# A third exponential, in place over the scores in PSUM, as the source of the remainder in the first layer

## The chip, the cores and the metric

The kernel runs on one core of one Trainium2 chip. The metric is device time in microseconds (us) for one execution of the whole program, as the median of several runs. The engines are named as the profile names them: PE (matmul) and PEld (the weight loads of the same engine), DVE (VectorE), ACT (ScalarE), POOL (GpSimd) and SP (which issues DMAs).

## The reference

One inference step of a two-layer encoder trunk, for a prompt of 2048 new frames and a sample of 32 frames. The first layer mixes tokens by attention within a band of 64-frame chunks, with a learned relative-position bias; the second by multi-head latent attention. The part that the change touches is the first layer's attention, 16 heads of 64:

```python
def attend(q, k, v, bias, mask, scale):
    s = jnp.einsum('bqhd,bkhd->bhqk', q, k).astype(jnp.float32) * scale
    if bias is not None:
        s = s + bias[None]
    s = jnp.where(mask[None, None], s, NEG_INF)
    p = jax.nn.softmax(s, axis=-1).astype(v.dtype)
    return jnp.einsum('bhqk,bkhd->bqhd', p, v)
```

A chunk sees itself and the eight chunks before it. All is float32, so the kernel splits every factor of a matmul in two float32r parts, a high one (the rounded value) and a low one (the remainder), and adds the products.

## The kernel before, in words

The first layer goes over 32 steps: two halves of the prompt, in each eight pairs of heads (`g`), for each pair two blocks of 512 queries (`blk`). A step handles two heads (`h`). Each head goes over tiles of 128 keys against up to 512 queries: four tiles (`c` = 1, of widths 512, 384, 256 and 128) in block 0, and eight in the later blocks, where four tiles of the block before come in (`c` = 0, of the same four widths). That makes 8 items in each of the 8 steps of block 0 and 16 in each of the other 24, 448 items in all, 112 of each width, 320 columns wide on average.

An item is made in `scores`. Two matmuls (L629 and L630) write the transposed scores into a PSUM bank; the tag `st` has two banks, bank_74 and bank_78, which items take in turn. The second matmul subtracts the row maximum, which `prep` found before. DVE adds the bias in place (L633, for some tiles L636) and masks a corner with a memset (L637). ACT then reads the bank twice: P = exp as float32 into SBUF (L643; for a head's first item straight into the sum `acc`) and Ph = exp rounded to float32r (L644). DVE forms the remainder Pl = P - Ph (L645) out of these two SBUF tiles, and POOL adds P to `acc` (L647) for all but a head's first item. P, Ph and Pl have three buffers each.

In `values`, two items later (`LAGA` = 2), one matmul multiplies Ph (L656) and one Pl (L657) by the values, into the one bank of the tag `av` (bank_94). After a head's last item `evac` takes that bank out (ACT L666, DVE L667) and folds the two halves of `acc` (DVE L668). `finish` makes the denominators: a matmul with `half_ones`, a product with 1 + exp(-z), and four reciprocals on DVE (L687), then two multiplications (L688, L689).

Beside these items stands the work for the next step: `project` and `project_z` (the matmuls of L189, L190 and L191), `prep` (transposes, the split of queries and keys by ACT L562 and L564 and DVE L566 and L567, the row maxima on DVE, L595 and L613), `finish` of the step before, and weight splits. A plan places them between the items in the program, and a scheduler then sets the order on each engine when the program is built: it goes by the program's order and by what is ready in its own account, so an instruction that waits longer there lets others pass. On the chip each engine runs its list in that order.

The buffers of P, Ph and Pl are named with numbers: P@63 to P@65, Ph@55 to Ph@57, Pl@58 to Pl@60; `acc` is acc@61 and acc@62.

Of the kernel before, what the change touches and what calls it, by code (L numbers as in the profile page):

```python
# [10 lines left out]
AF = mybir.ActivationFunctionType  # L11
ALU = mybir.AluOpType
# [19 lines left out]
def f32(ap):  # L32
    return ap if ap.dtype == F32 else ap.bitcast(F32)
# [6 lines left out]
def flip(t, c0, c1):  # L40

    n = t.shape[1]
    a = t[:, n - c1:n - c0]
    return bass.AP(a.tensor, a.offset + c1 - c0 - 1, [list(a.ap[0]), [-1, c1 - c0]])
# [55 lines left out]
def trunk(ctx: ExitStack, tc: tile.TileContext, I, O, stop=99):  # L100
    nc = tc.nc
    V, S, G, T = nc.vector, nc.scalar, nc.gpsimd, nc.tensor
# [90 lines left out]
    def bank(tag):  # L193
        order = psum[tag if tag in psum else "mx"]
        order.append(order.pop(0))
        return banks[order[-1]]
# [144 lines left out]
    def at1(shape, name, dt=F32, bufs=1):  # L341
        return at.tile(shape, dt, tag=name, name=name, bufs=bufs)
# [279 lines left out]
    def scores(s, h, n, c, t):  # L622
        blk, u = s["blk"], s[h]
        src = blk % 2 if c else 1 - blk % 2
        q0, w = (128 * t, 512 - 128 * t) if c else (0, 128 * t + 128)
        ks, qs = slice(128 * t, 128 * t + 128), slice(q0, q0 + w)
        bt = bias[s["g"], h][1]
        st = bank("st")
        T.matmul(st[:, 0:w], KA[h][src][:, ks], u["qa"][:, qs], start=True, stop=False)  # L629
        T.matmul(st[:, 0:w], KG[h][src][:, ks], u["qg"][:, qs], start=False, stop=True)  # L630
        if c:
            b1 = min(256, w)
            V.tensor_tensor(st[:, 0:b1], st[:, 0:b1], flip(bt, 0, b1), ALU.add)  # L633
        else:
            if t == 3:
                V.tensor_tensor(st[:, 0:128], st[:, 0:128], flip(bt, 128, 256), ALU.add)  # L636
            V.memset(st[0:64, w - 64:w], NEG)  # L637
        Ph = at1([128, 512], "Ph", F32R, PBUFS)
        Pl = at1([128, 512], "Pl", F32R, PBUFS)
        if n == 0:  # L640
            u["acc"] = at1([128, 512], "acc", bufs=2)
        P = at1([128, 512], "P", bufs=PBUFS) if n else u["acc"]
        S.activation(P[:, 0:w], st[:, 0:w], AF.Exp)  # L643
        S.activation(Ph[:, 0:w], st[:, 0:w], AF.Exp)  # L644
        V.tensor_tensor(Pl[:, 0:w], P[:, 0:w], f32(Ph[:, 0:w]), ALU.subtract)  # L645
        if n:
            G.tensor_tensor(u["acc"][:, qs], u["acc"][:, qs], P[:, 0:w], ALU.add)  # L647
        return Ph, Pl, w, qs, src
# [289 lines left out]
    for si, s in enumerate(steps):  # L938
# [55 lines left out]
        for i, (h, n, c, t) in enumerate(items):  # L994
            fifo.append((s, h, n, n == len(tiles) - 1, t, scores(s, h, n, c, t)))
            while plan and plan[0][0] <= (i + 1) / len(items):
                next(plan.pop(0)[1], None)
            if len(fifo) > LAGA:
                x = fifo.pop(0)
                values(*x)  # L1000
                if x[3]:
                    evac(x[0], x[1])
# [725 lines left out]
    for i in range(len(items) + LAG + 20):  # L1728
        if i < len(items):
            u, t = items[i]  # L1730
            fifo.append((u, t, scores(u, t)))
# [233 lines left out]
```

## Time and profile before

| what | us |
|---|---|
| median of 3 runs | 3829.01 |
| lowest, highest | 3823.49, 3842.70 |
| the profiled execution's own time | 3833.15 |
| its span, first to last instruction | 3831.0 |
| PE busy, all of the span | 3573.2 |
| DVE busy | 2996.9 |
| ACT busy | 1987.3 |
| POOL busy | 1629.8 |

The first layer's items run from about 130 to 1680 us of the span, and the rows below are nearly all of that stretch, called the stage. Two things have to be kept in mind when they are read. Matmuls are pipelined and their records overlap, so a busy PE is not PE at its peak. And a wait is put down to the semaphore that came last.

### The profile page before, as it was taken

Reading aid. Unit: us, or ns where it says so; the run is one execution under the profiler, and the core shown is the slowest. Engines: PE = TensorE matmul, PEld = TensorE weight load, DVE = VectorE, ACT = ScalarE, POOL = GpSimd, SP = SyncE. Lnnn points to the kernel's source line nnn. Section 1 sums busy time; section 2 is a strip of 40 time slices with the busy share of each in tenths; the row PEclk is TensorE's granted clock in tenths of the full one; section 3 lists DMA queues with packets and bytes.
Section 4 is the critical chain, followed back from the end, with each engine's and each line's share of the span. In section 5 each row is a group of like instructions: output and inputs, shape, how many; then the busy total and the mean of one; then the engine's idle time right before and its main releaser. Section 6 shows DMA issues by size and latency. Waiting matters only on the chain. (4 is left out here: it accounts for less than half of the span.)

```text
span 3831.0 us, 56760 instructions
## 1 busy us (share of the span) xinstructions
PE 3573.2 (93%) x17810; PEld 2892.2 (75%) x17810; DVE 2996.9 (78%) x6694; ACT 1987.3 (52%) x4790; POOL 1629.8 (43%) x1680
## 2 busy tenths in 40 slices
PE   7899999989999999889998999978999999998999
PEld 4678878777776667667887888857777787777887
DVE  4788888879988877877777766678888898885653
ACT  3544544555444434552223555546767677775542
POOL 0132222333333323541112444448788888885032
PEclk9899999989999999889999999979999999999999
DMA  5222222222223332343446476663332332333253
GB/s 172 68 60 59 65 77 67 72 70 67 64 82 98 105 89 76 98 145 123 132 132 209 143 203 195 189 166 112 90 92 70 96 89 74 81 84 107 86 178 126
DMA packets 441966, 412.85 MB, mean 108 GB/s; under 512 B 68809, under 2 KB 364285, under 8 KB 434625
## 3 DMA queue, kind: packets, MB, share of 16 engines
q1 hardware_dynamic: 441664, 409.23, 36.7%
q8 instruction: 141, 2.31, 0.3%
q14 instruction: 161, 1.31, 0.1%
HBM read 251.72 MB, written 140.10 MB: 102 GB/s over the span
## 5 line engine op out<-in xcount | busy, mean ns | idle before, releaser
L1513 DVE TENSOR_REDUCE mp@319_16907<-bank 128x1 f32<-128x512 f32 (+3 forms) x384 | 233.8, 615 | 28.6 <-PE bank L1512 26.4
L647 POOL TENSOR_TENSOR acc@61_858<-acc@61_858,P@63_885 128x256 f32<-128x256 f32 (+3 forms) x64 | 56.9, 889 | 215.0 <-ACT P@63_885 L643 111.0
L1513 DVE TENSOR_REDUCE mp@320_16908<-bank 128x1 f32<-128x512 f32 (+1 forms) x192 | 117.0, 613 | 16.8 <-PE bank L1512 16.4
L1546 ACT ACTIVATE P@430_22139<-bank 128x512 f32<-128x512 f32 (+2 forms) x156 | 83.3, 534 | 73.7 <-issue 38.0
L1546 ACT ACTIVATE P@432_22141<-bank 128x512 f32<-128x512 f32 (+2 forms) x156 | 83.2, 533 | 68.7 <-issue 34.0
L647 POOL TENSOR_TENSOR acc@61_858<-acc@61_858,P@64_886 128x256 f32<-128x256 f32 (+3 forms) x64 | 57.3, 895 | 143.9 <-ACT P@64_886 L643 104.7
L647 POOL TENSOR_TENSOR acc@61_858<-acc@61_858,P@65_887 128x128 f32<-128x128 f32 (+3 forms) x64 | 57.2, 894 | 143.4 <-ACT P@65_887 L643 98.5
L643 ACT ACTIVATE P@63_885<-bank 128x384 f32<-128x384 f32 (+3 forms) x128 | 52.8, 412 | 123.9 <-DVE bank L633 58.9
L687 DVE RECIPROCAL ez@69_1247<-ez@69_1247 128x128 f32<-128x128 f32 x128 | 115.9, 920 | 0.0
L643 ACT ACTIVATE P@65_887<-bank 128x128 f32<-128x128 f32 (+3 forms) x128 | 52.5, 410 | 117.8 <-DVE bank L637 59.6
L1546 ACT ACTIVATE P@429_22138<-bank 128x512 f32<-128x512 f32 (+2 forms) x156 | 83.5, 535 | 56.1 <-issue 12.7
L1546 ACT ACTIVATE P@431_22140<-bank 128x512 f32<-128x512 f32 (+2 forms) x156 | 83.5, 535 | 53.6 <-issue 11.3
L643 ACT ACTIVATE P@64_886<-bank 128x256 f32<-128x256 f32 (+3 forms) x128 | 52.4, 409 | 112.5 <-DVE bank L633 54.3
L647 POOL TENSOR_TENSOR acc@62_859<-acc@62_859,P@63_885 128x128 f32<-128x128 f32 (+3 forms) x64 | 58.3, 911 | 114.3 <-ACT P@63_885 L643 103.9
L647 POOL TENSOR_TENSOR acc@62_859<-acc@62_859,P@65_887 128x256 f32<-128x256 f32 (+3 forms) x64 | 55.2, 862 | 118.8 <-ACT P@65_887 L643 112.6
L647 POOL TENSOR_TENSOR acc@62_859<-acc@62_859,P@64_886 128x256 f32<-128x256 f32 (+3 forms) x64 | 55.6, 869 | 101.2 <-ACT P@64_886 L643 91.4
L149 POOL TENSOR_TENSOR ozl@169_14178<-ozl_@174_14186,ozh@167_14176 128x1024 fp32r<-128x1024 f32 x8 | 19.3, 2415 | 150.7 <-ACT ozh@167_14176 L148 150.7
L1563 DVE TENSOR_TENSOR bank<-bank,P@431_22140 128x512 f32<-128x512 f32 (+2 forms) x108 | 66.5, 616 | 11.6 <-ACT P@431_22140 L1546 10.8
L1563 DVE TENSOR_TENSOR bank<-bank,P@429_22138 128x512 f32<-128x512 f32 (+2 forms) x108 | 66.5, 616 | 7.9 <-ACT P@429_22138 L1546 7.1
L1547 ACT ACTIVATE Ph@421_22117<-bank 128x512 fp32r<-128x512 f32 (+1 forms) x128 | 72.7, 568 | 0.0
L595 DVE TENSOR_REDUCE md@50_694<-bank 128x1 f32<-128x384 f32 (+1 forms) x112 | 55.6, 516 | 21.5 <-PE bank L594 20.8
L1547 ACT ACTIVATE Ph@418_22114<-bank 128x512 fp32r<-128x512 f32 (+2 forms) x128 | 67.8, 530 | 4.0 <-DMA N<-hl@383_17303 4.0
(2155 smaller groups left out, 14843.9 us busy)
## 6 DMA issues: line engine op xcount, KB each, us to landing
h<-hT@197_14210 SPq DMA_DIRECT2D x16, 1024.0 KB
N<-hl@383_17303 SPq DMA_DIRECT2D x32, 512.0 KB
N<-hl@384_17304 SPq DMA_DIRECT2D x32, 512.0 KB
wr@10_289<-in_a_w_in SPq DMA_DIRECT2D x64, 192.0 KB
wr@11_290<-in_a_w_in SPq DMA_DIRECT2D x64, 192.0 KB
xr@9_224<-in_ada_w SPq DMA_DIRECT2D x32, 256.0 KB
xr@8_223<-in_ada_w SPq DMA_DIRECT2D x32, 256.0 KB
h1@214_14229<-h SPq DMA_DIRECT2D x8, 1024.0 KB
```

The source lines that it names most:

```text
L149: (eng or V).tensor_tensor(twin(nc, raw), raw, f32(hi), ALU.subtract)
L595: V.tensor_reduce(md[:, j:j + 1], X[:, 0:n], AX.X, ALU.max)
L643: S.activation(P[:, 0:w], st[:, 0:w], AF.Exp)
L647: G.tensor_tensor(u["acc"][:, qs], u["acc"][:, qs], P[:, 0:w], ALU.add)
L687: V.reciprocal(ez[:, cs], ez[:, cs])
L1513: V.tensor_reduce(mp[:, j, c:c + 1] if blk else m4[:, j:j + 1], X[:, 0:w], AX.X, ALU.max)
L1546: S.activation(P[:, 0:w], st[:, 0:w], AF.Exp)
L1547: S.activation(Ph[:, 0:w], st[:, 0:w], AF.Exp)
L1563: V.tensor_tensor((u["acc"] if last else u["sum"])[:, qs], old, P[:, 0:w], ALU.add)
```

## The change

One instruction is added for each item and one operand is replaced. After the two exponentials ACT makes a third one, in place: it reads the scores in the PSUM bank and writes their exponential back over them. DVE forms the remainder from there, as (bank) - Ph, in place of P - Ph. P itself is still made, and is read by POOL alone.

```diff
         S.activation(P[:, 0:w], st[:, 0:w], AF.Exp)
         S.activation(Ph[:, 0:w], st[:, 0:w], AF.Exp)
-        V.tensor_tensor(Pl[:, 0:w], P[:, 0:w], f32(Ph[:, 0:w]), ALU.subtract)
+        S.activation(st[:, 0:w], st[:, 0:w], AF.Exp)
+        V.tensor_tensor(Pl[:, 0:w], st[:, 0:w], f32(Ph[:, 0:w]), ALU.subtract)
         if n:
             G.tensor_tensor(u["acc"][:, qs], u["acc"][:, qs], P[:, 0:w], ALU.add)
```

The lines behind it move by one: the remainder is L646 in the changed kernel, POOL's addition L648, the two products of `values` L657 and L658.

The scheduler also sets another order around the items. On PE this is the place of the span's 452nd us, in the fifth pair's first step; the scores of bank_78 (L629 and L630) take the bank that the item of Ph@55 and Pl@58 had. Before:

```order
L189 MATMUL bank_70<-wq@13_294,HT1@4_119 128x384
L190 MATMUL bank_70<-wq@13_294,HT1@4_119 128x384
L191 MATMUL bank_70<-wq@13_294,HT1@4_119 128x384
L189 MATMUL bank_70<-wq@14_295,HT1@4_119 128x384
L629 MATMUL bank_78<-QA@45_606,KA11@27_560 128x128
L630 MATMUL bank_78<-QG@47_608,KG11@31_564 128x128
L656 MATMUL bank_94<-Ph@55_852,VT11@35_568 128x256
L657 MATMUL bank_94<-Pl@58_855,VT11@35_568 128x256
L629 MATMUL bank_74<-QA@44_605,KA00@24_557 128x512
```

The same place on PE in the changed kernel:

```order
L189 MATMUL bank_70<-wq@14_295,HT1@4_119 128x384
L657 MATMUL bank_94<-Ph@55_852,VT11@35_568 128x256
L190 MATMUL bank_70<-wq@14_295,HT1@4_119 128x384
L191 MATMUL bank_70<-wq@14_295,HT1@4_119 128x384
L189 MATMUL bank_70<-wq@15_296,HT1@4_119 128x384
L190 MATMUL bank_70<-wq@15_296,HT1@4_119 128x384
L629 MATMUL bank_78<-QA@45_606,KA11@27_560 128x128
L630 MATMUL bank_78<-QG@47_608,KG11@31_564 128x128
L658 MATMUL bank_94<-Pl@58_855,VT11@35_568 128x256
L629 MATMUL bank_74<-QA@44_605,KA00@24_557 128x512
```

The Ph product and four more projection matmuls now stand ahead of the scores that reuse the bank. On ACT, the same items. Before:

```order
L643 ACTIVATE P@65_887<-bank_78 128x256
L644 ACTIVATE Ph@55_852<-bank_78 128x256
L643 ACTIVATE P@63_885<-bank_74 128x128
L644 ACTIVATE Ph@56_853<-bank_74 128x128
L643 ACTIVATE P@64_886<-bank_78 128x128
L644 ACTIVATE Ph@57_854<-bank_78 128x128
L675 CAST ez_@70_1248<-pair@68_1079 128x512
```

ACT in the changed kernel:

```order
L643 ACTIVATE P@65_888<-bank_78 128x256
L644 ACTIVATE Ph@55_852<-bank_78 128x256
L645 ACTIVATE bank_78<-bank_78 128x256
L643 ACTIVATE P@63_886<-bank_74 128x128
L644 ACTIVATE Ph@56_853<-bank_74 128x128
L645 ACTIVATE bank_74<-bank_74 128x128
L643 ACTIVATE P@64_887<-bank_78 128x128
L644 ACTIVATE Ph@57_854<-bank_78 128x128
L645 ACTIVATE bank_78<-bank_78 128x128
L676 CAST ez_@70_1259<-pair@68_1085 128x512
```

The third exponential stands right behind the second, ahead of the next item's first. From the end of the first layer on, PE's order is the same in both kernels.

## Rows read from the trace of the kernel before

**Rows 1.** The stage and what follows: engine, busy us (instructions), clock, DMA share.
```profile
core 0: us, PE busy (x) PEld busy (x) DVE busy (x) ACT busy (x) POOL busy (x), PEclk, DMA share, GB/s
120.00:1680.00 1560.00, 1454.37 (x7055) 1154.37 (x7054) 1323.02 (x3186) 752.78 (x1840) 510.44 (x522) 0.94 0.28 78
1680.00:3831.00 2151.00, 2027.56 (x10400) 1682.54 (x10399) 1617.94 (x3345) 1183.52 (x2805) 1114.99 (x1149) 0.97 0.43 127
```
**Rows 2.** PE in a projection: start us, duration us.
```profile
459.02 0.33 PE L190 MATMUL bank<-wq@14_295,HT1@4_119 128*128 128x384 f32 x1
459.20 0.33 PE L191 MATMUL bank<-wq@14_295,HT1@4_119 128*128 128x384 f32 x1
459.37 0.33 PE L189 MATMUL bank<-wq@15_296,HT1@4_119 128*128 128x384 f32 x1
```
**Rows 3.** Slices of 8 us with DVE at 7.2 or more: first and last.
```profile
144.00:152.00 8.00, 6.88 (x37) 5.79 (x37) 7.21 (x15) 6.17 (x17) 4.90 (x5) 1.00 0.44 125
...
1672.00:1680.00 8.00, 3.77 (x11) 2.50 (x12) 7.93 (x5) 4.89 (x11) 6.19 (x5) 0.50 0.58 193
```
**Rows 4.** Busy time of one line alone: L645 (all, first such slice), L643.
```profile
core 0: us, DVE busy (x), PEclk, DMA share, GB/s
120.00:1690.00 1570.00, 323.98 (x448) 0.94 0.28 78
...
144.00:152.00 8.00, 1.49 (x2) 1.00 0.44 125
...
core 0: us, ACT busy (x), PEclk, DMA share, GB/s
120.00:1690.00 1570.00, 193.62 (x448) 0.94 0.28 78
```
**Rows 5.** DVE, subtractions and additions by line: ns min/median/max, first and last start.
```profile
L645 DVE TENSOR_TENSOR Pl@59_856<-acc@62_859,Ph@56_853 x21: 670/691/1624, 139.6 to 1583.1; 128x512 fp32r<-128x512 f32 x21
L567 DVE TENSOR_TENSOR KA00@24_557<-bank,KA00@24_557 x16: 693/693/694, 85.4 to 1541.3; 64x512 fp32r<-64x512 f32 x16
L1563 DVE TENSOR_TENSOR bank<-P@432_22141,P@429_22138 x12: 884/1240/1367, 2563.8 to 3291.7; 128x384 f32<-128x384 f32 x12
```
**Rows 6.** DVE groups by form: busy us, mean ns, idle before.
```profile
L645 DVE TENSOR_TENSOR Pl@59_856<-P@63_885,Ph@56_853 128x384 fp32r<-128x384 f32 x20 | 18.2, 909 | 0.7 <-ACT Ph@56_853 L644 0.3
L633 DVE TENSOR_TENSOR bank<-bank,BT0@38_581 128x256 f32<-128x256 f32 x48 | 20.5, 427 | 9.5 <-PE bank L630 9.3
L633 DVE TENSOR_TENSOR bank<-bank,BT0@38_581 128x128 f32<-128x128 f32 x16 | 4.6, 290 | 0.0
```
**Rows 7.** Four engines at the place whose order stands above.
```profile
452.03 0.38 ACT L643 ACTIVATE P@65_887<-bank 128x256 f32<-128x256 f32 x1 [2.10 <-DVE bank L637]
...
452.31 0.38 ACT L644 ACTIVATE Ph@55_852<-bank 128x256 fp32r<-128x256 f32 x1
...
452.49 0.73 POOL L647 TENSOR_TENSOR acc@62_859<-acc@62_859,P@65_887 128x256 f32<-128x256 f32 x1 [1.97 <-ACT P@65_887 L643]
...
452.72 0.78 DVE L645 TENSOR_TENSOR Pl@58_855<-P@65_887,Ph@55_852 128x256 fp32r<-128x256 f32 x1 [0.47 <-ACT Ph@55_852 L644]
...
452.74 0.19 PEld L629 LDWEIGHTS bank<-QA@45_606,KA11@27_560 128*128 128x128 f32 x1 [0.24 <-ACT Ph@55_852 L644]
...
452.91 0.28 PE L630 MATMUL bank<-QG@47_608,KG11@31_564 65*128 65x128 f32 x1
...
453.56 0.39 PE L657 MATMUL bank<-Pl@58_855,VT11@35_568 128*128 128x256 f32 x1 [0.21 <-DVE Pl@58_855 L645]
```
**Rows 8.** Waits in the stage: who waited for whom, us in total, times, longest.
```profile
POOL acc@61_858 L647 <- DVE Pl@60_857 L645: 81.0, 12, 17.7
PEld bank L629 <- ACT Ph@57_854 L644: 17.9, 27, 2.8
PE bank L656 <- DVE ob@66_1077 L667: 15.8, 8, 2.9
PE bank L591 <- DMA QG@46_607<-QA@44_605: 13.4, 11, 1.5
PEld bank L629 <- ACT Ph@56_853 L644: 10.4, 28, 1.0
PEld bank L657 <- DVE Pl@60_857 L645: 9.6, 22, 0.9
PEld bank L657 <- DVE Pl@58_855 L645: 7.2, 16, 1.2
PEld bank L629 <- ACT Ph@55_852 L644: 5.2, 16, 0.7
```
**Rows 9.** ACT by line, out of PSUM and into it: ns min/median/max.
```profile
L643 ACT ACTIVATE acc@62_859<-bank x32: 580/598/607, 137.8 to 1649.1; 128x512 f32<-128x512 f32 x32
L314 ACT ACTIVATE bank<-x@163_14171 x12: 597/602/607, 1698.1 to 2036.5; 128x512 f32<-128x512 f32 x12
```

## The prediction

> **What bounds the kernel now.** I first read the stage's sums, since the change ends with the first layer: the order on PE is the same in both kernels from 1680 us on, and the 2151 us behind that point [rows 1] are left alone. In the stage of 1560 us PE is busy for 1454, DVE for 1323, ACT for 753 and POOL for 510 [rows 1]. By these sums PE would be the bound, with 106 us to gain at most. But in a run of projections a 384-wide matmul starts every 0.17 to 0.18 us and is recorded with 0.33 [rows 2], so records overlap two deep, and a PE that does half its rate still looks full. [...]
>
> Then I cut the stage in slices of 8 us. In 93 of 195 slices DVE is busy for 7.2 us or more [rows 3], 744 us in all, and ACT, summed over the same slices, for half of the time. DVE instructions stand one behind the other there; that is where a cheaper DVE instruction moves the end. In the other 102 slices the stage runs on latencies: PE stands in its order before scores, Ph or Pl products or a landed DMA [rows 8].
>
> **The change part by part.** *The remainder on DVE.* L645 costs 324 us for 448 items [rows 4], 723 ns each. It reads two SBUF tiles, and such instructions spread widely: 670 at best, 691 in the median and 1624 at worst for 512 columns; another line with two SBUF inputs takes 884 to 1367 for only 384 [rows 5]. In the place of rows 7 it takes 0.78 us for 256 columns while POOL's addition, also out of SBUF, runs over its start. DVE instructions with one input in PSUM do not spread: L567 (bank minus SBUF into SBUF as float32r, exactly the new form, on 64 partitions) takes 693, 693 and 694 [rows 5]. So I price the new remainder at 693 ns for 512, 427 for 256 and 290 for 128 columns [rows 5, 6], and 560 for 384, midway between 427 and 693. With 112 items of each width that is 112 x 1970 ns = 221 us, 103 us (32%) less. The bounds: nothing, if the spread came from something else than the second SBUF input, and all of the 103 us.
>
> [...]
>
> What reaches the end is the share in the full slices. L645 is busy there for 165 us, summed over the 93 slices [rows 3, 4], and 32% of that is 53 us. I take **-53 us**, between 0 (PE takes over as the bound at once) and -103 (DVE decides everywhere).
>
> *The third exponential on ACT.* It has the shape of L643, 194 us in all [rows 4]. Out of PSUM into SBUF 512 columns take 598 ns, and an activation into PSUM 602 [rows 9], so 190 to 200 us are added and ACT goes from 753 to about 950 us of 1560, 61%. ACT stays far from the bound. In its queue the next item's P waits 0.3 us longer behind it (two exponentials of 0.38 us start 0.28 apart [rows 7]), and so do the copies of `prep`, 64 of each kind (16 for each of four buffers, as their DVE partner L567 [rows 5]), one of which sends the DMA that PE's L591 waits for [rows 8]. At 0.28 us for each of 64 that is 18 us at most; DVE's shorter queue hides most of it. I take **+5**, between 0 and 18.
>
> *The bank.* The scores that reuse a bank waited for Ph; now they wait for the remainder. In the place of rows 7 Ph ends at 452.69 and L629 starts at 452.74. With the third exponential the scores are free at about 452.97, and a remainder of 0.43 us on a free DVE ends at 453.45, so L629 could start 0.76 us later. In the stage 71 weight loads of L629 waited for Ph, 33.5 us together [rows 8]; 71 x 0.76 = 54 us if the order had stayed. It did not: at this place the Ph product and four projection matmuls now stand ahead of L629, and four times 0.17 us [rows 2] and the product cover the 0.76. And the Pl product right behind these scores waited for the same remainder anyway, until 453.56 [rows 7]; two of its three wait groups come to 16.8 us [rows 8], and these disappear when L629 has waited already. I take **+8**, between -10 and +54.
>
> *Gone with the change.* POOL no longer waits until DVE has read `acc`, 81 us in one pair of buffers alone [rows 8]; POOL is busy a third of the stage and nobody is held up by it there, so this is worth nothing. P's three buffers come free at POOL's addition, as most did. What the new wait queues up: the remainder waits on DVE for one more exponential, and behind it the next item's bias or row maximum; 0.28 us, where the remainder itself becomes 0.3 us shorter. That cancels.
>
> **The sum** is -53 + 5 + 8 = -40 us on the profiled execution's own time of 3833.15: **3793 us**. That execution lies 4 us above the median of 3829.01, within the runs' spread, so I leave the number at 3793. A measurement can tell about 0.5% from no change, 19 us.
>
> **The rivals.** *PE's own order is the bound.* If the full slices of DVE are full because PE lets them be, only waits that name DVE's queue shorten: L656 behind L667 (15.8 us in one buffer, two buffers), the Pl products, together some 50 us, of which a third, 17, goes. Less the 13 us of the two costs, that is 3829: no change. For it: PE is busy at 90% in the full slices too. Against it: PE's records overlap [rows 2].
>
> *Two banks are too few.* An item now holds its bank through scores (0.45 us [rows 7]), bias (0.43 [rows 6]), three exponentials 0.28 apart (0.94) and a remainder (0.43), 2.25 us, and it stands twice in DVE's queue. With one DVE instruction of average length, 1323 us / 3186 = 0.42 [rows 1], ahead of it each time that is 3.1 us for two banks, 1.55 us an item. Before it was 1.1 less a pair, 1.0 an item. The stage gives an item 1560/448 = 3.5 us on average, so this decides only where items stand closer than 1.55 us, between heads' heavy stretches. If half of the 448 items run in such bursts and each loses 0.3 us, that costs 67 us; the gain, halved, is 27: 3873, slower. For it: 71 of 448 scores already wait for their bank. Against it: the order now puts other matmuls between them.
>
> *The change doesn't do what it says*: if the remainder out of PSUM is as slow as before, the two costs are left, 3846, within 0.5%. L567's rows speak clearly against it.
>
> **How the numbers follow.** The forecast (DVE's full slices shorten) has 0.50, PE's order 0.24, two banks 0.21, no cheaper remainder 0.05. The forecast's own range is 3750 to 3815, from three quarters of the 103 us down to a third of the 53; one part in ten of it falls inside 0.5%. That gives faster 0.47 (0.45 of the forecast, 0.02 of the PE case), same 0.32, slower 0.21. For 8 times in 10 the range runs from 3750 to 3855: below are 0.05, above about 0.13.
>
> **What would show it.** Right: the remainder's line falls from 324 to about 221 us, with 512 columns steady near 693 ns; fewer than 93 slices of 8 us with DVE at 7.2 or more; L629's waits, now for the remainder, stay near 33 us; ACT near 950 us in the stage. Wrong: the stage keeps its 1560 us although DVE's busy time falls by 100 (PE's order), or L629 waits for the remainder for over 80 us (two banks).

## The result, and the profile of the changed kernel

The changed kernel takes 3764.53 us in the median of four runs (3761.46 to 3772.23). The kernel before, run beside it, takes 3826.25. The ratio is 0.9836 with an interval of 0.980 to 0.9871: 1.6% faster, some 60 us. The forecast was 3793, so the sign and the range held and the gain was half as large again as the sum gave. One execution of a later series of the changed kernel ran at a granted clock of 0.74 and took 4227.56 us; it is left out of that series' numbers.

The profiled execution takes 3772.23 us with a span of 3770.5, against 3833.15 and 3831.0 before. The page of the changed kernel, engines over the span:

```profile
span 3770.5 us, 57293 instructions
## 1 busy us (share of the span) xinstructions
PE 3531.8 (94%) x17810; PEld 2868.2 (76%) x17810; DVE 2903.5 (77%) x6694; ACT 2138.8 (57%) x5238; POOL 1598.0 (42%) x1680
```

The same two stretches as in [rows 1]; the stage now ends 60 us earlier, at 1620:

```profile
core 0: us, PE busy (x) PEld busy (x) DVE busy (x) ACT busy (x) POOL busy (x), PEclk, DMA share, GB/s
120.00:1620.00 1500.00, 1408.17 (x7049) 1127.64 (x7048) 1231.29 (x3189) 902.42 (x2284) 474.27 (x520) 0.96 0.29 81
1620.00:3771.00 2151.00, 2030.99 (x10401) 1685.15 (x10401) 1615.28 (x3338) 1184.82 (x2808) 1119.40 (x1150) 0.97 0.43 127
```

What follows the stage takes 2151 us in both kernels, so the whole gain lies in the stage. DVE has 92 us less to do there. ACT has 150 more and is busy for 60% of it.

The third exponential is L645, and evac's instruction on `ob` is L668 here. The remainder (L646) alone over the stage, then its instructions (ns min/median/max), then ACT's third exponential and its first:

```profile
core 0: us, DVE busy (x), PEclk, DMA share, GB/s
120.00:1690.00 1570.00, 216.21 (x448) 0.96 0.30 86
...
L646 DVE TENSOR_TENSOR Pl@58_855<-bank,Ph@55_852 x150: 216/425/693, 129.9 to 1617.4; 128x256 fp32r<-128x256 f32 x45, 128x512 fp32r<-128x512 f32 x38, 128x128 fp32r<-128x128 f32 x38, 128x384 fp32r<-128x384 f32 x29
...
core 0: us, ACT busy (x), PEclk, DMA share, GB/s
120.00:1690.00 1570.00, 200.36 (x448) 0.96 0.30 86
...
120.00:1690.00 1570.00, 193.28 (x448) 0.96 0.30 86
```

The remainder fell from 324 us [rows 4] to 216, and the longest of any width is 693 ns where [rows 5] has 1624. The third exponential is 200 us of new work on ACT. ACT's busy time rises by only 150, for the records of neighbouring exponentials overlap (0.38 us long and 0.28 apart in [rows 7]).

The waits that answer to [rows 8], in the stretch of the items:

```profile
PEld bank L629 <- DVE Pl@59_856 L646: 28.4, 28, 2.9
PEld bank L629 <- DVE Pl@60_857 L646: 25.9, 33, 2.3
PEld bank L629 <- DVE Pl@58_855 L646: 15.5, 21, 3.3
...
PE bank L657 <- DVE ob@66_1083 L668: 1.7, 1, 1.7
```

Two things have changed places. The scores now wait for the remainder, 70 us of weight loads in 82 waits, where 33.5 us in 71 waits went to Ph [rows 8]. But the wait of a head's first Ph product for evac's read of `ob` is nearly gone, 1.7 us. Before, this wait was 15.8 us in one buffer of `ob` [rows 8] and 11.7 us in the other:

```profile
PE bank L656 <- DVE ob@67_1078 L667: 11.7, 13, 2.0
```

### The profile page after: what moved, and what is told of

The parts are those of the page before. It is cut to its first block, busy times and chain, and to the rows that moved or that the text cites. A ratio compares the mean times of both kernels' runs of the same rounds, so it can differ in the third digit from the quotient of the medians.

```text
span 3770.5 us, 57293 instructions
## 1 busy us (share of the span) xinstructions
PE 3531.8 (94%) x17810; PEld 2868.2 (76%) x17810; DVE 2903.5 (77%) x6694; ACT 2138.8 (57%) x5238; POOL 1598.0 (42%) x1680
## 5 line engine op out<-in xcount | busy, mean ns | idle before, releaser
L645 ACT ACTIVATE bank<-bank 128x512 f32<-128x512 f32 x448 | 200.4, 447 | 0.0
L648 POOL TENSOR_TENSOR acc@61_858<-acc@61_858,P@63_886 128x256 f32<-128x256 f32 (+3 forms) x64 | 52.2, 816 | 212.5 <-ACT P@63_886 L643 172.2
L648 POOL TENSOR_TENSOR acc@61_858<-acc@61_858,P@64_887 128x256 f32<-128x256 f32 (+3 forms) x64 | 52.4, 819 | 154.0 <-ACT P@64_887 L643 122.1
L643 ACT ACTIVATE P@63_886<-bank 128x384 f32<-128x384 f32 (+3 forms) x128 | 52.7, 412 | 102.7 <-DVE bank L637 55.5
L648 POOL TENSOR_TENSOR acc@61_858<-acc@61_858,P@65_888 128x128 f32<-128x128 f32 (+3 forms) x64 | 51.7, 809 | 129.3 <-ACT P@65_888 L643 104.5
L648 POOL TENSOR_TENSOR acc@62_859<-acc@62_859,P@65_888 128x256 f32<-128x256 f32 (+3 forms) x64 | 54.5, 851 | 117.6 <-ACT P@65_888 L643 110.1
L643 ACT ACTIVATE P@65_888<-bank 128x128 f32<-128x128 f32 (+3 forms) x128 | 52.4, 410 | 88.1 <-DVE bank L637 45.4
L643 ACT ACTIVATE P@64_887<-bank 128x256 f32<-128x256 f32 (+3 forms) x128 | 52.4, 409 | 86.6 <-DVE bank L637 45.6
L648 POOL TENSOR_TENSOR acc@62_859<-acc@62_859,P@63_886 128x128 f32<-128x128 f32 (+3 forms) x64 | 54.9, 858 | 105.7 <-ACT P@63_886 L643 102.0
L648 POOL TENSOR_TENSOR acc@62_859<-acc@62_859,P@64_887 128x256 f32<-128x256 f32 (+3 forms) x64 | 54.2, 846 | 95.8 <-ACT P@64_887 L643 95.4
L646 DVE TENSOR_TENSOR Pl@58_855<-bank,Ph@55_852 128x512 fp32r<-128x512 f32 (+3 forms) x150 | 71.5, 477 | 21.5 <-ACT bank L645 20.3
L646 DVE TENSOR_TENSOR Pl@60_857<-bank,Ph@57_854 128x384 fp32r<-128x384 f32 (+3 forms) x149 | 72.2, 484 | 19.4 <-ACT bank L645 17.0
L646 DVE TENSOR_TENSOR Pl@59_856<-bank,Ph@56_853 128x384 fp32r<-128x384 f32 (+3 forms) x149 | 73.1, 491 | 17.6 <-ACT bank L645 15.4
L1564 DVE TENSOR_TENSOR bank<-bank,P@431_22588 128x512 f32<-128x512 f32 (+2 forms) x108 | 66.5, 616 | 12.3 <-ACT P@431_22588 L1547 11.5
```

The source lines that it names most:

```text
L645: S.activation(st[:, 0:w], st[:, 0:w], AF.Exp)
L646: V.tensor_tensor(Pl[:, 0:w], st[:, 0:w], f32(Ph[:, 0:w]), ALU.subtract)
L1564: V.tensor_tensor((u["acc"] if last else u["sum"])[:, qs], old, P[:, 0:w], ALU.add)
```

## The experiments

A gain of 60 us that may have two causes in it had to be taken apart. The theory was that the remainder is dear because POOL reads SBUF at the same time, and that an input from PSUM takes it out of that. The main rival was that the longer hold of the bank makes the scheduler write another order for PE, and that this order brings the gain. How far the order had moved is read from PE's weight loads: before, in 3 of the 448 items the scores of only one later item stood ahead of an item's Ph product, and those of two or three in nearly all others; in the changed kernel 193 items have only one ahead.

### Third exponential and bank held, remainder still out of two SBUF tiles

```diff
-        V.tensor_tensor(Pl[:, 0:w], st[:, 0:w], f32(Ph[:, 0:w]), ALU.subtract)
+        V.scalar_tensor_tensor(Pl[:, 0:w], P[:, 0:w], st[:, 0:1], f32(Ph[:, 0:w]), ALU.max, ALU.subtract)
```

> The changed kernel, but the remainder has two SBUF inputs again: max(P, s) - Ph, where s is one column of the exponentials in the bank (so its values are not the remainder's). The bank is held as long, ACT has its third exponential, the scheduler's order is nearly the changed kernel's. Theory A (the gain is the remainder's price: two SBUF inputs are held up while POOL's addition reads SBUF, a PSUM input is not): the remainder's line goes from 216 us back to 310 to 330, and the time to the before kernel's or above it, 3815 to 3860. Rival B (the gain is the scheduler's other order around the items): the remainder becomes dearer, but the time stays at 3760 to 3785.

It took 3803.46 us, ratio 0.996 [0.9941, 0.998]: a gain of 15 to 20 us. The order is much that of the changed kernel (198 items with only one ahead). The remainder's line, and the longest waits of PE's weight loads for it:

```profile
core 0: us, DVE busy (x), PEclk, DMA share, GB/s
120.00:1690.00 1570.00, 319.01 (x448) 0.96 0.29 81
...
PEld bank L629 <- DVE Pl@60_857 L646: 44.5, 59, 2.6
PEld bank L629 <- DVE Pl@59_856 L646: 34.2, 41, 2.7
PEld bank L629 <- DVE Pl@58_855 L646: 26.4, 32, 4.2
```

With the second input in SBUF the line costs 319 us again, and the scores wait 105 us for it. From here to the changed kernel, where only the second input moves into PSUM, it is another 34 to 47 us (by the medians of its two series, and by the ratios). So the larger part of the gain belongs to the remainder's price, and a smaller one exists without it.

### The third exponential alone, unread

The changed kernel with the remainder out of P, as before; the bank is then held to the third exponential only.

```diff
-        V.tensor_tensor(Pl[:, 0:w], st[:, 0:w], f32(Ph[:, 0:w]), ALU.subtract)
+        V.tensor_tensor(Pl[:, 0:w], P[:, 0:w], f32(Ph[:, 0:w]), ALU.subtract)
```

> The third exponential is made in the bank, but nothing reads it: the remainder is P - Ph out of SBUF as before. Theory A: the cost of the third exponential alone, +0 to +20 us on the before kernel: 3826 to 3846; the remainder's line stays at 310 to 330 us. Rival B (the order and the longer hold of the bank make the gain): 3765 to 3800.

3837.71 us, ratio 1.0039 [1.0023, 1.0056]: 14 us slower. PE waits for evac as it did before:

```profile
PE bank L657 <- DVE ob@67_1084 L668: 15.7, 12, 2.3
PE bank L657 <- DVE ob@66_1083 L668: 14.2, 9, 3.1
```

Here the order moved part of the way (134 items with one ahead), and nothing was gained. The third exponential is no gift; what the kernel above has over this one, 34 us, comes with the hold of the bank to the remainder.

### The hold without the third exponential

The kernel before, in which the remainder also reads one column of the bank. Where that score lies above P the remainder has another value, against what was expected.

```diff
-        V.tensor_tensor(Pl[:, 0:w], P[:, 0:w], f32(Ph[:, 0:w]), ALU.subtract)
+        V.scalar_tensor_tensor(Pl[:, 0:w], P[:, 0:w], st[:, 0:1], f32(Ph[:, 0:w]), ALU.max, ALU.subtract)
```

> The before kernel, with the remainder as max(P, s) - Ph, where s is one column of the bank's masked scores, none of them above P: the same values, two SBUF inputs as before and no third exponential, but the bank is now held until the remainder, and the scheduler orders PE for that (the Ph product stands ahead of the scores that are two items later in 163 of 448 places, in the before kernel in 4). If that order is worth the 34 us between the two kernels with a third exponential and a remainder out of SBUF: 3785 to 3805, the remainder's line still at 310 to 330 us. If the 34 us come only together with ACT's third exponential, or the hold of the bank costs: 3824 to 3850.

3802.73 us, ratio 0.9947 [0.9907, 0.9986]: 21 us faster than the kernel before, though its remainder was the dearest of all.

```profile
core 0: us, DVE busy (x), PEclk, DMA share, GB/s
120.00:1690.00 1570.00, 336.39 (x448) 0.96 0.29 82
...
PE bank L656 <- DVE ob@67_1078 L667: 5.8, 10, 0.8
PE bank L656 <- DVE ob@66_1077 L667: 3.5, 5, 1.2
```

So the kernel in which the bank is held longer is faster by about 0.5%. The hold by itself can only add waits, so the gain must come with the order that the scheduler then writes (162 items with one ahead): PE's wait for evac falls from 27.5 us to 9. It comes out level with the first experiment, which has the third exponential on top: in this order the exponential costs nothing that can be measured.

### The cheap remainder without the third exponential

The changed kernel without L645; the remainder takes the maximum of bank and Ph, so it has the new form and the new hold, but other values.

```diff
-        S.activation(st[:, 0:w], st[:, 0:w], AF.Exp)
-        V.tensor_tensor(Pl[:, 0:w], st[:, 0:w], f32(Ph[:, 0:w]), ALU.subtract)
+        V.tensor_tensor(Pl[:, 0:w], st[:, 0:w], f32(Ph[:, 0:w]), ALU.max)
```

> The before kernel, in which the remainder's place is taken by max(scores, Ph) out of the bank (its values are not the remainder's, and the third exponential is left out). Theory A with the third exponential as a cost: the remainder's line at about 216 us, ACT back at about 750 us in the stage, and the time 5 to 25 us below the changed kernel's: 3740 to 3760. Rival (ACT has room and the bank, not ACT, is what the change costs): within 5 us of the changed kernel, 3760 to 3770.

3761.83 us, ratio 0.9839 [0.9804, 0.9874], level with the changed kernel. The scores wait half as long for the remainder (34 us of weight loads), and it brings nothing. The 200 us on ACT are hidden. Against the kernel with the hold alone, whose order is nearly this one (162 items with one ahead there, 156 here), only the form of the remainder differs, and that is worth 41 us by the medians and by the ratios. This is the cleanest measure here of the cheap remainder at two banks.

### Both kernels without POOL's additions

The sums for the denominators are left out, in both: P has its own tile for every item, and POOL does not add it.

```diff
-        P = at1([128, 512], "P", bufs=PBUFS) if n else u["acc"]
+            G.memset(u["acc"], 1.0)
+        P = at1([128, 512], "P", bufs=PBUFS)
...
-        if n:
-            G.tensor_tensor(u["acc"][:, qs], u["acc"][:, qs], P[:, 0:w], ALU.add)
```

The kernel before with this edit:

> The before kernel without POOL's additions to the sum (POOL fills the sum with ones instead, so the denominators are left out). Theory A: without POOL's reads of SBUF the remainder, still out of SBUF, falls from 324 to about 221 us by itself, and the time by at least what the change brought: 3740 to 3775. Rival B: the remainder may become cheaper, but the order is nearly the before kernel's: 3805 to 3830.

The changed kernel with it:

> The changed kernel without POOL's additions to the sum (the denominators are left out). Theory A: the remainder stays at about 216 us, nothing is left for the change to win, and its third exponential and longer hold of the bank remain: 0 to 25 us slower than the before kernel without the additions. Rival B: the order's gain is still there, 40 to 60 us faster than the before kernel without the additions.

3736.27 us, ratio 0.9768 [0.9746, 0.9789], for the one and 3744.52, ratio 0.979 [0.9768, 0.9811], for the other. The remainder out of two SBUF tiles, in the kernel before without the additions:

```profile
core 0: us, DVE busy (x), PEclk, DMA share, GB/s
120.00:1690.00 1570.00, 224.56 (x448) 0.97 0.31 89
```

The remainder out of PSUM, in the changed kernel without them:

```profile
core 0: us, DVE busy (x), PEclk, DMA share, GB/s
120.00:1690.00 1570.00, 215.90 (x448) 0.96 0.31 88
```

Nothing was done to the remainder in the kernel before, and its order around the items is that of before (3 items with one ahead), yet the line falls from 324 to 225 us. So 99 of the 108 us by which the line stood above its price out of PSUM come with POOL's additions. With them gone the change has nothing left to win: it is 8 us slower than the kernel before with the same edit, by the medians, and the two intervals overlap. Without the additions the program gains 88 us where it had the dear remainder and 20 to 25 where it had the cheap one. In which way POOL's additions hold up a remainder out of two SBUF tiles was not shown; that they do, with 99 us on this line, is what the pair shows.

### Three banks for the scores

One bank is taken from the tag `mx`, in both kernels.

```diff
-    psum_pool(mm=2, st=2, mx=3, av=1)
+    psum_pool(mm=2, st=3, mx=2, av=1)
```

The changed kernel with it, and a second series of this kernel and of the changed kernel side by side:

> The changed kernel with three PSUM banks for the scores in place of two; prep and finish get two in place of three. If the longer hold of the bank costs: L629's waits for the remainder (72 us of its weight loads) fall below 25 us, and the time to 3735 to 3760. If the bank costs nothing at the end, or prep misses its third bank more: 3765 to 3800.

> The changed kernel with three banks for the scores and two for prep and finish once more. If the hold of the bank costs at the end: 5 to 15 us below the changed kernel of the same call; if not, within 5 us.

> The changed kernel once more, beside the next one on the same chip: 3755 to 3775.

The kernel before with it:

> The before kernel with the same three banks for the scores and two for prep and finish. Its scores waited for Ph for 33 us, less than the changed kernel's for the remainder, so it should win less than the changed kernel does, or lose more: if the bank's hold is a cost of the change, the difference between the two kernels grows from 62 to 75 to 90 us.

| kernel | banks | us | ratio to before |
|---|---|---|---|
| before | 3 | 3833.16 | 1.0022 [0.9995, 1.0048] |
| changed | 3 | 3755.44 | 0.9821 [0.9778, 0.9863] |
| changed, second series | 3 | 3756.47 | 0.9814 [0.9782, 0.9845] |
| changed, second series | 2 | 3769.29 | 0.9849 [0.9802, 0.9896] |

The longest waits of the scores for the remainder, changed kernel with three banks:

```profile
PEld bank L629 <- DVE Pl@59_856 L646: 6.0, 5, 3.6
...
PEld bank L629 <- DVE Pl@58_855 L646: 2.3, 4, 0.9
...
PEld bank L629 <- DVE Pl@60_857 L646: 1.5, 2, 0.9
```

The 70 us of waiting become 10, and the time falls by 9 and by 13 us in the two series (by 6 and 13 by the ratios). The intervals overlap, so the size is not sure; both series have the same sign, and this is the fastest version that does all of the work. The third bank brings the kernel before nothing, although it takes away all of the 33.5 us that its scores waited for Ph [rows 8]. So the sum of such waits is not time that can be won.

The two kernels with three banks are a second way to take the change apart, because here the order is nearly the same in both: the item's Ph product stands behind the scores of exactly two later items in 392 of 448 items of the one and in 406 of the other. Third exponential and remainder together are worth 78 us between them.

### Two exponentials, and two additions on POOL

P is dropped; the remainder comes out of PSUM, and POOL adds Ph and Pl to the sums instead of P.

```diff
-    PBUFS = 3
+    PBUFS = 4
...
-        P = at1([128, 512], "P", bufs=PBUFS) if n else u["acc"]
-        S.activation(P[:, 0:w], st[:, 0:w], AF.Exp)
...
+        acc = u["acc"][:, qs]
...
-            G.tensor_tensor(u["acc"][:, qs], u["acc"][:, qs], P[:, 0:w], ALU.add)
+            G.tensor_tensor(acc, acc, f32(Ph[:, 0:w]), ALU.add)
+            G.tensor_tensor(acc, acc, f32(Pl[:, 0:w]), ALU.add)
+        else:
+            G.tensor_tensor(acc, f32(Ph[:, 0:w]), f32(Pl[:, 0:w]), ALU.add)
```

> The changed kernel without P: ACT makes Ph and then the exponential in place, DVE forms the remainder from the bank, and POOL adds Ph and the remainder to the sum in two additions (four buffers of Ph and of the remainder, none of P). ACT is back at about 710 us in the stage and the remainder comes 0.3 us earlier; POOL's additions go from 320 to about 640 us of 1500. If ACT's third exponential is a cost at the end: 3740 to 3760. If POOL's second addition holds up the other DVE instructions with two SBUF inputs, or the sum comes too late for the end of a head: 3770 to 3800.

3824.01 us, ratio 0.9999 [0.9979, 1.0019]: the whole gain is gone. POOL over the stage, then the remainder:

```profile
core 0: us, POOL busy (x), PEclk, DMA share, GB/s
120.00:1700.00 1580.00, 907.30 (x979) 0.94 0.28 80
...
core 0: us, DVE busy (x), PEclk, DMA share, GB/s
120.00:1700.00 1580.00, 211.90 (x448) 0.94 0.28 80
```

The remainder is as cheap as in the changed kernel, so a cheap remainder alone is no promise of a faster program. Where the time goes is seen when the items are split at the first scores of the second half of the prompt. The last stretch ends with the last scores. In the traces of the kernel before and of the changed one the granted clock is recorded as 1.0 or as 0.5; the time at 0.5 is worked out from the mean clock, in the same way for all six:

| kernel | first half, us | of it at clock 0.5 | second half, us | of it at clock 0.5 |
|---|---|---|---|---|
| before | 734 | 72 | 847 | 126 |
| changed | 720 | 31 | 808 | 94 |
| third exponential and hold | 735 | 34 | 826 | 82 |
| third exponential alone | 767 | 108 | 816 | 86 |
| hold alone | 736 | 44 | 812 | 72 |
| this kernel | 772 | 116 | 803 | 72 |

All five kernels whose order moved are 21 to 44 us shorter in the second half. The two that gain nothing in total, this one and the third exponential alone, lose 38 and 33 us in the first half, and they have 44 and 36 us more at clock 0.5 there than the kernel before. Inside the first half the changed kernel stays at 1.0 from 250 to 720 us, and this kernel does not. The changed kernel, then this one, with one fall and the wait in front of it:

```profile
core 0: us, PE busy (x), PEclk, DMA share, GB/s
250.00:720.00 470.00, 444.36 (x2410) 1.00 0.23 63
...
250.00:720.00 470.00, 444.00 (x2277) 0.95 0.22 61
410.00:420.00 10.00, 7.41 (x41) 1.00 0.26 76
420.00:430.00 10.00, 9.60 (x30) 0.61 0.42 122
...
420.40 0.72 PE L591 MATMUL bank<-KG00@28_561,QG@46_607 64*128 64x384 f32 x3 [2.91 <-DMA QG@46_607<-QA@44_605]
```

PE stands for 2.91 us until the DMA that brings `QG` has landed, and behind that the clock falls to 0.61 over 10 us. Over the stage PE waits 18 us for this DMA in L591, where the changed kernel has 8 and the kernel before 13 [rows 8]. What holds the DMA and the other waits up, POOL's second addition or another part of the edit, was not taken apart.

## Why the prediction was right, point by point

**What bounds the stage.** That DVE's queue decides in a part of the stage, and that PE's busy share says little, held: DVE lost 92 us of work and the stage lost 60, while PE is busy for 93% of the stage before and for 94% of it now. Of the 195 slices of 8 us, 66 now have DVE at 7.2 us or more, where the prediction counts 93 [rows 3]. The first and the last within the items of the changed kernel:

```profile
core 0: us, PE busy (x) PEld busy (x) DVE busy (x) ACT busy (x) POOL busy (x), PEclk, DMA share, GB/s
136.00:144.00 8.00, 7.42 (x42) 6.38 (x40) 7.46 (x18) 7.43 (x20) 3.17 (x4) 1.00 0.46 133
...
1608.00:1616.00 8.00, 3.60 (x12) 2.39 (x11) 7.93 (x15) 3.62 (x9) 3.04 (x3) 0.71 0.25 65
```

**The remainder.** Its price was forecast from L567 and from the by-form rows as 221 us, and 216 were measured: 5 us below the forecast, and 512 columns never took more than 693 ns. Without POOL's additions, too, the form with a PSUM input takes 216 us and the one with two SBUF inputs 225.

**The step that failed** depends on the route by which the change is taken apart, and so its place among two terms stays open. By the kernels with three banks it is the share of these 103 us that reaches the end. I counted the line's time only in slices with DVE at 7.2 us or more, which gave 53. Where the order hardly moves, with three banks, the change is worth 78 us, third exponential included, so some three quarters arrived. The same working with slices of 6.4 us and more (137 of them hold 250 us of the line) gives 80; but this bound is chosen after the fact. By the kernels with two banks the cheap remainder is worth 34 to 47 us, a little less than the 53, and the failed term is the bank's: +8 was forecast where hold and order together bring 15 to 21 us of gain. That the time fell inside the range although the bank's term had the wrong sign by this route is in part luck. The range itself was drawn wide: three quarters of 103 us less the two costs of 13 gives 3769 and not 3750. The changed kernel's profiled 3772.23 would still lie inside.

**The third exponential.** Its size was right, 200 us for 190 to 200. The +5 is within what the runs leave: +14 where it is added alone, nothing that can be measured where the new order stands.

**The bank.** Three banks against two give +9 and +13 for the wait, close to the +8. But L629's waits did not stay near 33 us: they are 70, and by the two series with three banks most of that is covered by other work. That the sizes are alike is then in part luck. What I had not priced is the order itself. With three banks the whole is 78 less 9 to 13, and the third bank itself cost the kernel before 5 to 8; with two banks the parts, 15 to 21 and 34 to 47, give 49 to 68. The totals agree and the parts differ. The runs fit with both parts relieving the same thing: in the order of before PE stood for 27.5 us at a head's first Ph product until DVE's queue had reached evac, and that wait is all but gone in the changed kernel and much shorter with the hold alone. It is not the whole, for the kernel with two additions on POOL has only 3.5 us of it left and gains nothing. The exponential alone, which moved the order part of the way, has 29.9 us of it; it gains 31 us in the second half and loses 33 in the first. Why the longer hold leads the scheduler to the better order was not settled.

**The granted clock** had no term in the sum, and it moved. Its mean over these 1570 us was 0.94 [rows 4] and is 0.96; in the two profiles that is 197 us at clock 0.5 before and 126 now. In the slice at 1608 us shown above PE is busy for 3.60 of 8 us and the clock falls to 0.71. What such time costs can be estimated from executions of the kernel before alone: one with a mean clock of 0.966 took 3800.12 us and one with 0.954 took 3841.53, which is 41 us for 95 more at clock 0.5. At this rate the 71 us less would be some 30 of the 60 gained, and the 85 us by which the kernel with two additions on POOL exceeds the changed one in the first half some 37 of the 52 lost there. These are estimates, and the clock may be no cause beside the others: in the row shown it falls behind a wait of PE of 2.91 us. Whether such waits bring the falls about was not shown. In the first experiment and in the one with the hold alone the clock is 0.96 too, and they gain only 20 us, so the clock does not explain the rest.

**The rivals.** PE's own order as the bound is refuted: it forecast 3829. "Two banks are too few" was right about the waits, 82 of them, and wrong about their price: 9 to 13 us, not 67. That the remainder would be no cheaper is refuted by its line. POOL's waits for `acc` went as described, 81 us in one pair [rows 8], and next to nobody had waited for them: DVE waited 1.1 us for POOL where it folds `acc`. In the changed kernel that is 13.0 us in 19 waits, a small cost that was not forecast.

## What to carry to other kernels

When a DVE instruction with two SBUF inputs spreads as the remainder did here (670 to 1624 ns for 512 columns [rows 5]), look for work of POOL out of SBUF beside it. In this kernel one input in PSUM took the spread out (at most 693 ns), and it can pay to compute that input a second time on an engine with room, here ACT, busy for 60% of the stage with it. Measure both kernels with the other engine's work left out, too: here that alone gave more than the change (88 us against 60), and with it the change gave nothing. And where a scheduler writes the order, a longer hold of a buffer is an edit to the order too, to be priced by itself. When such an order gains in one stretch and loses in another, compare the granted clock of the stretches before a cause is named.

## What the runs showed of the hardware

A DVE subtraction out of PSUM and SBUF took at most 694 ns in any of 448 items of up to 512 columns, beside POOL's additions or not (216 us with them, 215.90 without); the same out of two SBUF tiles took 324 us beside them and 225 without. Without the additions POOL still had other work (226 us from 120 to 1620 us, in the kernel before with that edit), and single instructions with two SBUF inputs still reached 1770 ns. An exponential in place in PSUM was not cheaper than one into SBUF, 200 us against 193 for the same 448 shapes. With two additions on POOL, busy for 907 of 1580 us and still idle for two fifths, the whole gain of 60 us was gone, though the remainder was as cheap; by which way was not shown. And a wait of PE of 2.91 us stood in front of a fall of the granted clock to 0.61 over 10 us.
